# Decode trunk step on one core: key pages of heads 4-7 by plain loads, the other gathers in pairs with time between, GpSimd held to its place

## The chip, the cores and the metric

The kernel is one program on 1 core of one Trainium2 chip. The metric is its time on the device in microseconds (us), from three timed runs; beside them stands one execution that the hardware profiler recorded. In what follows PE is the matmul engine (TensorE), PEld its weight loads, DVE the vector engine, ACT the scalar engine, POOL GpSimd and SP the engine that issues most of the transfers.

## What is computed

One step of a decoder layer, for a prompt of 512 tokens and for 8 samples of 4 tokens, with shared weights in float32. One projection feeds two groups of 8 heads. Group A is native sparse attention (NSA): compressed blocks, selected blocks and a window. Group B is forgetting attention ("fox"). The samples have 1024 past rows each, held in pages of 128 rows that a page table names.

```python
h = rmsnorm(x, norm_in)
q_n, kv_n, gates, z_n, q_f, k_f, v_f, logf, z_f = project(h, w_in, b_gate, b_forget)
...
past_nsa = cache_nsa_kv[page_table].reshape(B, P, 4, NSA_KV_HEADS, HEAD_DIM)
nsa_all = jnp.concatenate([past_nsa, kv_n[:, :, :4]], axis=1)
kc, c_end = compress(nsa_all[:, :, 0], cmp_pe[0], cmp_w[0])
vc, _ = compress(nsa_all[:, :, 1], cmp_pe[1], cmp_w[1])
...
past_fox = cache_fox_kv[page_table].reshape(B, P, 2, FOX_HEADS, HEAD_DIM)
k_all = jnp.concatenate([past_fox[:, :, 0], k_f], axis=1)
v_all = jnp.concatenate([past_fox[:, :, 1], v_f], axis=1)
o_f = fox_block(q_f, q_pos, d_all[:, P:], k_all, v_all, d_all, jnp.arange(P + T))
...
y = x + einsum(concat(o_n * silu(z_n), o_f * silu(z_f)), w_out)
```

## The kernel before

**Tiles and stages.** The projection runs over 61 column tiles of 128 columns (`run_tiles`). Each takes 96 matmuls into the PSUM tiles `pz`: float32 is made of three products of rounded parts, weights `whi` and `wlo` times input `h_hi` and `h_lo`. A weight quarter arrives as `raw` (256 KB, five buffers), ACT writes `whi` from it and DVE writes `wlo`. After the last tile comes the output projection (`run_outputs`, tile `po`), which takes the 16 mixed heads one after the other.

**Streams.** Everything else is a set of generators (`Streams`) that put their instructions between the projection's matmuls. While the program is built, a model of the five engines (`Clock`) keeps a time for each. `pump`, called after every third matmul, lets each generator go on whose last yield is met: a list of tiles that are ready by the model, a flag, or a function. So the order of every engine is fixed when the program is built, and on the chip the engines meet by semaphores alone. `calm` holds a stream back until the model's DMA queue is short.

**The streams that the change touches.** `fox_sample(hh)` handles heads 0-3 (hh = 0), then heads 4-7 (hh = 1). Its `pager` fills pages `fpg` (128 partitions, 4 x 512 elements, two buffers): first 16 key pages, then 16 value pages. A key page is four gathers, each an indirect DMA of 128 rows of 512 elements that POOL issues with indices from `fi`; the gather puts row i + 32a of sample b in partition 32b + i and quarter a. DVE transposes the page into `ft`, and PE makes scores in `accv`. A value page is four plain loads by `load_page`, whose page number comes from a register; samples with an even number go over SP's queue, those with an odd one over POOL's. `compress` makes the compressed keys and values of the samples' pages: `load_rows(u)` gathers 16 sets of rows `crow` (four gathers each, two buffers), set u + 2 as soon as set u has been transposed into `ct`. `nsa()` runs `compress`, `nsa_prompt` and `nsa_sample` in this order; `nsa_sample` loads its pages `spg` in the same way as value pages.

**POOL's queue.** After the index arithmetic POOL issues nothing but gathers and its half of the plain loads. A gather waits on the chip only for its buffer (read by DVE) and, at the start, for one weight quarter (the copy into `gone`). Nothing else ties it to the place that the model gave it.

Of the kernel before, what the change touches and what calls it, by code (L numbers as in the profile page):

```python
# [23 lines left out]
TOK = 544  # L24
FPG = 2
CALM = 4.0
HALF_D = 1024
T_WIN = 28
SETS = 5
# [202 lines left out]
class Streams:  # L232
# [3 lines left out]
    def __init__(self, clock):  # L236
        self.clock = clock
        self.items = []
        self.flags = set()
        self.left = {"tr": 2, "nat": 2}  # L240

    def add(self, gen, front=False, filler=False):
        s = dict(gen=gen, flags=(), at=0.0, test=None, filler=filler)
# [51 lines left out]

    def calm(self, us):
        return lambda: self.clock.queued() <= us

    def after(self, us):
        until = self.clock.t["pe"] + us  # L300
# [28 lines left out]
def dram(ap, offset, dims):  # L329
    return bass.AP(tensor=ap.tensor, offset=ap.offset + offset, ap=dims)  # L330
# [3 lines left out]
def trunk_step(ctx, tc, x_prompt, x_sample, cache_nsa_kv, cache_fox_kv, cache_fox_logf, state_nsa_win,  # L334
# [16 lines left out]
    def gate(side):  # L351
        return lambda: clock.t["pe"] >= clock.gate.get(side, 0.0)
# [98 lines left out]
    nc.vector.memset(ones, 1.0)  # L451
    bias32 = cst.tile([P, 32], F32, name="bias32")
    w_0 = {}


    h_hi = keep.tile([P, KT, TOK], F32R, name="h_hi")
    h_lo = keep.tile([P, KT, TOK], F32R, name="h_lo")
# [468 lines left out]
    def gather(t, tab, idx):  # L926
        nc.gpsimd.indirect_dma_start(out=t, out_offset=None, in_=tab,
                                     in_offset=bass.IndirectOffsetOnAxis(ap=idx, axis=0))
# [191 lines left out]
    def fox_sample(hh):  # L1120
# [7 lines left out]
        def pager():  # L1128
            while at[0] < len(seq):
                yield lambda: at[0] < at[1] + FPG  # L1130
                yield S.calm(CALM)
                kv, bq, kb = seq[at[0]]
                pages[at[0]] = pg = fx.tile([P, 4, 512], F32, name="fpg", bufs=FPG)
                for b in range(4):
                    if kv:
                        load_page(pg[:, b], cache_fox_kv, (bq * 4 + b) * 8 + kb,
                                  lambda c: c[0, :, 1, hs, :].rearrange("p h d -> p (h d)"))
                    else:
                        gather(pg[:, b], dram(cache_fox_kv, 0, [[512, n_pool * 512], [1, 512]]),
                               IX["f"][hh][:, bq * 8 + kb, b:b + 1])  # L1140
                at[0] += 1

        if hh == 0:
            yield ("idx", "x15")
            first = raws[3 + W_RAW]
            yield [first]
            nc.gpsimd.tensor_copy(IX["gone"], first[:, 3, P - 1:])
        S.add(pager())
        qb = fx.tile([P, 4, 4, 64], F32, name="fqb")
        nc.vector.memset(qb, 0.0)  # L1150
# [148 lines left out]
    def compress(pl):  # L1299
# [5 lines left out]
        S.put_nat()  # L1305
        gs, cw = {}, {}

        def load_rows(u):
            if u < 16:
                cg, bh = divmod(u, 2)  # L1310
                gs[u] = pl.tile([P, 4, 512], F32, name="crow", bufs=2)
                for b in range(4):
                    gather(gs[u][:, b], nsa_tab, IX["c"][:, bh * 4 + b, cg:cg + 1])

        def load_w(s):
            if s < 32:
                cg, kv, dp = s // 4, s // 2 % 2, s % 2
                cw[s] = t = pl.tile([P, 2, P], F32, name="cw", bufs=3)
                for d in range(2):
                    load(t[:, d], dram(cmp_w, (kv * 32 + cg * 4) * P * P + (dp * 2 + d) * 32 * P, [[P * P, 4], [P, 32], [1, P]]))  # L1320
        load_rows(0)
        load_w(0)
        load_w(1)
        more = []
        for kv in range(2):
# [13 lines left out]
                                  peT[:, :, kv * 8:kv * 8 + 8].rearrange("p d g -> p g d"))  # L1339
            nc.vector.transpose(m[:, :, :32], cz.rearrange("p g d -> p (g d)"))  # L1340
            yield
        load_rows(1)
        WIDE = 256 + MORE
        pss = [s_tile([P, WIDE]) for _ in range(2)]
        psb = psum.tile([P, 2, 256], F32, name="psb", tag="acc", bufs=1)
# [8 lines left out]
        for step in steps + [None]:  # L1354
            if step:
                cg, bh, kv, dp = step
                u, s = cg * 2 + bh, cg * 4 + kv * 2 + dp
                if bh == 0:
                    load_w(s + 2)
                    yield [cw[s]]  # L1360
                    ws[kv, dp] = pair(pl, [P, 2, P], "cwx", 4)
                    yield from split((*ws[kv, dp], cw.pop(s)))
                n = 256 if bh else WIDE
                X = [x[:, :, :n] for x in pair(pl, [P, 2, WIDE], "cx", 3)]
                yield [gs[u]]
                t = pl.tile([P, 2, WIDE], F32, name="ct", bufs=2)[:, :, :n]
                if bh == 0:
                    cp(t[:, :, 256:], more[kv][:, cg * 4 + dp * 2:cg * 4 + dp * 2 + 2, :])
                nc.vector.transpose(t[:, :, :256].rearrange("p c (a i) -> p a c i", i=32),
                                    gs[u].rearrange("p b (k v d) -> p b k v d", k=2, v=2)[:, :, kv, :, dp * 64:dp * 64 + 64])  # L1370
                yield
                if kv and dp:
                    gs.pop(u)
                    load_rows(u + 2)
                yield from split((*X, t))
                now = step, ws[kv, dp], X
            if prev:
                at, w, x = prev
                for c in range(2):
                    yield [x[1], w[1]]  # L1380
                    products(*at, c, w, x)
            prev = now
# [679 lines left out]
    def index_tiles():  # L2062
# [52 lines left out]
        nc.gpsimd.tensor_scalar(cb_, cb_, 2.0, None, op0=OP.mult)  # L2115
        nc.gpsimd.tensor_tensor(at, steps[:, None, :].to_broadcast([P, 8, 8]), cb_[:, :, None].to_broadcast([P, 8, 8]), op=OP.add)
        nc.gpsimd.tensor_copy(IX["c"], at)
        IX["gone"] = fsk.tile([P, 1], F32, name="gone")
        p2 = IX["p2"] = fsk.tile([64, 2], I32, name="pid2")
        for x in range(2):  # L2120
            nc.gpsimd.tensor_scalar(p2[:, x:x + 1], pid, 2.0, float(x), op0=OP.mult, op1=OP.add)
# [16 lines left out]
    if True:  # L2138
        fsk = pool("fsk")
        fxk = ctx.enter_context(tile_pool("fxk", **side))  # L2140
        fxs = ExitStack()
        fx = fxs.enter_context(tile_pool("fx", **side))
        qs_f = fxk.tile([P, 8, 32], F32, name="qs_f")
        ks_f = fxk.tile([P, 8, 32], F32, name="ks_f")
        ptrow = fsk.tile([1, 64], I32, name="ptrow")

        def nsa():
            yield ("idx", "started", "places")
            with tile_pool("phc") as pl:
                yield from compress(pl)  # L2150
            yield gate("left")
            with tile_pool("phn") as pl:
                yield from nsa_prompt(pl)
            yield gate("left")
            with tile_pool("phs") as pl:
                yield from nsa_sample(pl)
            yield gate("left")
            pl = ctx.enter_context(tile_pool("mxp"))
            MX.update(mx=by_rows(pl.tile([P, 16, TOK], F32, name="mx")), pl=pl, kept=set(), free=4)
            flags.add("mx")  # L2160

        def fox():
            pn = []
            for hh in range(2):
                pn.append((yield from fox_sample(hh)))
            fxs.close()
            yield gate("right")
            with tile_pool("phf", **side) as pl:
                for hh in range(2):
                    S.add(new_values(pl, hh, pn[hh]))  # L2170
                yield from fox_prompt(pl)
                yield ("foxs0", "foxs1")
            flags.add("fox")

        S.add(index_tiles(), front=True)
        S.add(start(), front=True)
        S.add(places())
        S.add(fox_sample_setup())
        S.add(fox())
        S.add(nsa())  # L2180
        for hd in range(16):
            S.add(mix(hd))
            S.add(turn_in(hd))
        S.add(last_stage())
        run_tiles(0, n_in)
        flags.add("in_done")
        S.need("mx")
# [28 lines left out]
```

## Time and profile before

| | us |
|---|---|
| median of 3 runs | 1327.93 (1327.69 to 1328.9) |
| profiled execution | 1329.99 |
| its span, first to last instruction | 1328.3 |
| PE busy in the span | 1272.8 |
| mean granted clock of PE | 0.979 |

PE's two clock states in this trace are full (1.0) and half; the profile's rows give the mean over a stretch. "Busy" of PE counts pipelined matmuls, so a busy PE is not always one at its peak. An idle stretch is put down to the engine or transfer that ended it; "issue" means that the profile shows nothing it waited for.

### The profile page before, as it was taken

How to read it: one execution, taken by the hardware profiler on the slowest of the kernel's cores; microseconds unless marked ns; L12 is line 12 of the kernel's file. 1: busy time of each engine (PE TensorE's matmuls, PEld its weight loads, DVE VectorE, ACT ScalarE, POOL GpSimd, SP SyncE). 2: the span in 40 equal slices, each digit the busy share in tenths (PEclk: the TensorE clock that was granted, in tenths of full speed). 3: DMA queues.
4: the chain of work that ended last, by engine and by line, in shares of the span. 5: the costliest groups of instructions: out<-in, count | busy, mean ns of one | idle time of the engine just before them, and what ended most of it. 6: DMA issues, size and time to landing. Idle time of an engine off the chain costs nothing.

```text
span 1328.3 us, 27189 instructions
## 1 busy us (share of the span) xinstructions
PE 1272.8 (96%) x10097; PEld 1144.2 (86%) x10097; DVE 785.4 (59%) x1979; ACT 540.6 (41%) x1164; POOL 286.1 (22%) x377
## 2 busy tenths in 40 slices
PE   8899988888999999999999999999999999999997
PEld 6899968878988988888998889979899899777786
DVE  6545746666764457767565554876586437345255
ACT  5323312322343224545355553557567524333221
POOL 6400354455241134444001111011200100000000
PEclk9999988899999989999999999999999999999999
DMA  8655767678687888776946878796977785434423
GB/s 212 208 120 138 210 198 217 204 218 235 206 272 230 276 249 253 237 238 209 267 102 192 229 232 188 187 221 194 286 206 183 219 295 170 129 108 132 138 74 135
DMA packets 308053, 266.30 MB, mean 200 GB/s; under 512 B 87174, under 2 KB 255062, under 8 KB 307248
## 3 DMA queue, kind: packets, MB, share of 16 engines
q1 hardware_dynamic: 283968, 188.60, 50.4%
q0 software_dynamic: 23904, 75.84, 18.0%
q8 instruction: 79, 1.29, 0.4%
q14 instruction: 54, 0.44, 0.1%
q10 hardware_dynamic: 48, 0.13, 0.0%
HBM read 236.04 MB, written 36.77 MB: 205 GB/s over the span
## 4 chain that ended last, share of the span: by engine, by line
PE 86%; DVE 3%; issue 3%; DMA 3%; ACT 2%; another core or an unknown queue 2%; SPq 1%; DVEq 0%; ACTq 0%
PE pz L195 51%; PE po L195 15%; PE s L195 5%; PE tr L195 5%; PE accv L195 4%; PE acc L195 3%; PE psb L195 2%; PE accf L195 1%; SPq L195 1%; DVE ft L195 1%; DMA spg<-in_state_nsa_win 1%; DMA raw<-in_w_in 1%; DMA xt<-in_x_prompt 1%; ACT np L195 1%
## 5 line engine op out<-in xcount | busy, mean ns | idle before, releaser
L195 PE MATMUL pz<-h_hi,whi 128*128 128x272 f32 x1920 | 569.0, 296 | 16.6 <-ACT zt L195 9.8
L195 PE MATMUL pz<-h_hi,wlo 128*128 128x272 f32 x1920 | 559.3, 291 | 5.9 <-issue 5.9
L195 PE MATMUL pz<-h_lo,whi 128*128 128x272 f32 x1920 | 559.0, 291 | 5.4 <-issue 5.1
L195 PEld LDWEIGHTS pz<-h_hi,whi 128*128 128x128 f32 x1920 | 367.1, 191 | 31.3 <-issue 18.8
L195 PEld LDWEIGHTS pz<-h_lo,whi 128*128 128x128 f32 x1920 | 367.2, 191 | 9.1 <-issue 8.4
L195 PEld LDWEIGHTS pz<-h_hi,wlo 128*128 128x128 f32 x1920 | 366.9, 191 | 8.1 <-issue 8.0
L195 DVE TENSOR_TENSOR wlo<-raw,whi 128x512 fp32r<-128x512 f32 x275 | 186.3, 679 | 144.1 <-ACT whi L195 137.5
L195 ACT ACTIVATE whi<-raw 128x512 fp32r<-128x512 f32 x275 | 170.8, 625 | 246.3 <-PE pz L195 132.4
L195 POOL DMA_INDIRECT fpg<-in_cache_fox_kv,fi x128 | 131.1, 1024 | 163.8 <-DVE ft L195 97.5
L195 DVE TENSOR_TENSOR zt<-pz,rsb 128x272 f32<-128x272 f32 x86 | 37.9, 440 | 151.6 <-PE pz L195 139.3
L195 POOL DMA_INDIRECT crow<-in_cache_nsa_kv,ci x64 | 66.4, 1038 | 141.2 <-DVE qs_f L195 72.7
L195 PE MATMUL po<-whi,h_hi 128*128 128x512 f32 (+1 forms) x256 | 95.5, 373 | 0.0
L195 PE MATMUL po<-whi,h_lo 128*128 128x512 f32 (+1 forms) x256 | 93.5, 365 | 0.0
L195 PE MATMUL po<-wlo,h_hi 128*128 128x512 f32 (+1 forms) x256 | 93.4, 365 | 0.0
L195 DVE STREAM_TRANSPOSE ft<-fpg 128x1024 f32<-128x1024 f32 x64 | 78.9, 1235 | 9.9 <-remote 5.0
L195 POOL DMA_DIRECT2D spg<-in_cache_nsa_kv x64 | 34.9, 546 | 228.4 <-DVE skt L195 99.3
L195 POOL DMA_DIRECT2D fpg<-in_cache_fox_kv x64 | 34.7, 542 | 223.7 <-PE accv L195 172.0
L195 ACT ACTIVATE cxh<-ct 128x580 fp32r<-128x580 f32 (+1 forms) x64 | 42.1, 658 | 90.1 <-DVE ct L195 53.3
L195 PEld LDWEIGHTS po<-whi,h_hi 128*128 128x128 f32 x256 | 48.1, 188 | 19.7 <-ACT whi L195 7.5
L195 PEld LDWEIGHTS po<-whi,h_lo 128*128 128x128 f32 x256 | 48.2, 188 | 8.5
L195 PEld LDWEIGHTS po<-wlo,h_hi 128*128 128x128 f32 x256 | 48.2, 188 | 7.7
L195 DVE TENSOR_TENSOR cxl<-ct,cxh 128x580 fp32r<-128x580 f32 (+1 forms) x64 | 46.0, 719 | 12.4 <-ACT cxh L195 8.1
(411 smaller groups left out, 1874.3 us busy)
## 6 DMA issues: line engine op xcount, KB each, us to landing
raw<-in_w_in SPq DMA_DIRECT2D x240, 256.0 KB
fpg<-in_cache_fox_kv SPq DMA_DIRECT2D x64, 256.0 KB
fpg<-in_cache_fox_kv POOLq DMA_DIRECT2D x64, 256.0 KB
raw<-in_w_out SPq DMA_DIRECT2D x40, 256.0 KB
spg<-in_cache_nsa_kv POOLq DMA_DIRECT2D x64, 128.0 KB
spg<-in_cache_nsa_kv SPq DMA_DIRECT2D x64, 128.0 KB
out<-in_state_nsa_win SPq DMA_DIRECT2D x32, 254.0 KB
scr_z<-zt SPq DMA_DIRECT2D x28, 272.0 KB
```

The source lines that it names most:

```text
L195: return fn(*a, **k)
```

## The change

Key pages of heads 4-7 come by `load_page`: four loads of 32 partitions x 4 x 512 elements, which put the same rows in the same places. `calm` now holds back only the pages of heads 4-7. The gathers that remain (key pages of heads 0-3 and the rows of `compress`) come in pairs. Ahead of each pair stands `S.spaced`: it lets the pair in when the model's PE time is at least 2.8 us after the pair before, rows of `compress` ahead of key pages, and then calls `mark(j)`, which lets ACT write one column of `tick` and POOL copy it into `gone`. So POOL waits for ACT before each pair. `load_rows` becomes a stream of its own, `rows_in`. `nsa_sample` now also waits for the flag "sampled", set when both halves of the fox sample are done.

```diff
+SPACE = 2.8
...
+    def spaced(self, first=False):
+        self.ahead += first
+        yield lambda: self.clock.t["pe"] >= self.spaced_at and (first or not self.ahead)
+        self.ahead -= first
+        self.spaced_at = self.clock.t["pe"] + SPACE
+        j = self.gathers % 8
+        self.gathers += 1
+        self.mark(j)
...
+    tick = cst.tile([P, 8], F32, name="tick")
+    gone = cst.tile([P, 8], F32, name="gone")
+    clock.parts[tick.tensor.name] = clock.parts[gone.tensor.name] = (8, 1)
+
+    def mark(j):
+        cp(tick[:, j:j + 1], ident[:, j:j + 1])
+        nc.gpsimd.tensor_copy(gone[:, j:j + 1], tick[:, j:j + 1])
+    S.mark = mark
...
         def pager():
             while at[0] < len(seq):
                 yield lambda: at[0] < at[1] + FPG
-                yield S.calm(CALM)
+                if hh:
+                    yield S.calm(CALM)
...
+                    elif hh:
+                        load_page(pg[b * 32:b * 32 + 32], cache_fox_kv, (bq * 4 + b) * 8 + kb,
+                                  lambda c: c[0, :, 0, hs, :].rearrange("(a i) h d -> i a (h d)", i=32))
                     else:
+                        if b % 2 == 0:
+                            yield from S.spaced()
                         gather(pg[:, b], dram(cache_fox_kv, 0, [[512, n_pool * 512], [1, 512]]),
                                IX["f"][hh][:, bq * 8 + kb, b:b + 1])
...
-        def load_rows(u):
-            if u < 16:
+        done = [0]
+
+        def rows_in():
+            for u in range(16):
+                yield lambda: u < done[0] + 2
                 cg, bh = divmod(u, 2)
-                gs[u] = pl.tile([P, 4, 512], F32, name="crow", bufs=2)
+                rows = pl.tile([P, 4, 512], F32, name="crow", bufs=2)
                 for b in range(4):
-                    gather(gs[u][:, b], nsa_tab, IX["c"][:, bh * 4 + b, cg:cg + 1])
+                    if b % 2 == 0:
+                        yield from S.spaced(True)
+                    gather(rows[:, b], nsa_tab, IX["c"][:, bh * 4 + b, cg:cg + 1])
+                gs[u] = rows
...
+                yield lambda: u in gs
                 yield [gs[u]]
...
                     gs.pop(u)
-                    load_rows(u + 2)
+                    done[0] += 1
...
+            yield "sampled"
...
+            flags.add("sampled")
```

How this moves instructions is shown at three places. The first is POOL's queue in the first part of the program, where the pages of heads 0-3 and the rows of `compress` are gathered. Before (`fpg` key pages, `crow` rows of `compress`, `fi_248` and `ci` their indices):

```order
L195 COPY gone<-raw 128x1
L195 DMA fpg<-in_cache_fox_kv,fi_248 128x512 x8
L195 DMA crow<-in_cache_nsa_kv,ci 128x512 x16
L195 DMA fpg<-in_cache_fox_kv,fi_248 128x512 x8
L195 DMA crow<-in_cache_nsa_kv,ci 128x512 x4
```

And now, from the first gathers after the 16 of `crow` on (`tick` is written by ACT):

```order
L196 COPY gone<-tick 128x1
L196 DMA fpg<-in_cache_fox_kv,fi_250 128x512 x2
L196 COPY gone<-tick 128x1
L196 DMA fpg<-in_cache_fox_kv,fi_250 128x512 x2
L196 COPY gone<-tick 128x1
L196 DMA crow<-in_cache_nsa_kv,ci 128x512 x2
```

Eight and four gathers in a row have become twos, with a copy that waits for ACT before each.

The second place is ACT's queue in the same part of the program, now (`cxh` and `cwxh` are the rounded parts of `compress`, `ct` its transposed rows, `zt` a finished projection tile):

```order
L196 ACTIVATE tick<-ident 128x1
L196 ACTIVATE zt<-pz 128x272
L196 ACTIVATE cxh<-ct 128x580
L196 ACTIVATE tick<-ident 128x1
L196 ACTIVATE whi<-raw 128x512
L196 ACTIVATE cwxh<-cw 128x256
```

The ticks stand between the splits of weights and rows, so each is reached only when ACT has done the ones before it; before, the same operations stood there without them.

The third place is SP's queue where the sample's scores of heads 4-7 begin (`fss` is loaded for their softmax, `nat` holds stored rows). Before:

```order
L195 DMA fss<-scr_f 128x1x1024
L195 DMA scr_z<-zt 128x544
L195 DMA raw<-in_w_in 128x4x128 x2
L195 DMA out<-nat 4x32x32
L195 DMA out<-nat 32x16x32
```

And now:

```order
L196 DMA fss<-scr_f 128x1x1024
L196 ISA
L196 DMA fpg<-in_cache_fox_kv 32x4x512
L196 ISA
L196 DMA fpg<-in_cache_fox_kv 32x4x512
L196 DMA raw<-in_w_in 128x4x128
L196 DMA out<-in_state_nsa_win 16x4064
```

Two loads of each key page of heads 4-7 now stand in SP's queue ahead of weights (ISA sets up the register with the page's number); the other two stand in POOL's, where there were 64 gathers in a row.

More of the change, by code (lines that the diff above doesn't have):

```diff
@@ L240, in __init__ @@
         self.left = {"tr": 2, "nat": 2}
+        self.gathers, self.spaced_at, self.ahead = 0, 0.0, 0
     def add(self, gen, front=False, filler=False):
@@ L1146, in fox_sample @@
             yield [first]
-            nc.gpsimd.tensor_copy(IX["gone"], first[:, 3, P - 1:])
+            nc.gpsimd.tensor_copy(gone[:, :1], first[:, 3, P - 1:])
         S.add(pager())
@@ L1320, in load_w @@
                     load(t[:, d], dram(cmp_w, (kv * 32 + cg * 4) * P * P + (dp * 2 + d) * 32 * P, [[P * P, 4], [P, 32], [1, P]]))
-        load_rows(0)
+        S.add(rows_in())
         load_w(0)
@@ L1341, in compress @@
             yield
-        load_rows(1)
         WIDE = 256 + MORE
@@ L2117, in index_tiles @@
         nc.gpsimd.tensor_copy(IX["c"], at)
-        IX["gone"] = fsk.tile([P, 1], F32, name="gone")
         p2 = IX["p2"] = fsk.tile([64, 2], I32, name="pid2")
```

## Prediction, made before the change was run

> **What bounds the kernel now.** I read the page's head and chain first, to see which engine sets the end.
>
> ```profile
> PE 1272.8 (96%) x10097; PEld 1144.2 (86%) x10097; DVE 785.4 (59%) x1979; ACT 540.6 (41%) x1164; POOL 286.1 (22%) x377
> PEclk9999988899999989999999999999999999999999
> PE 86%; DVE 3%; issue 3%; DMA 3%; ACT 2%; another core or an unknown queue 2%; SPq 1%; DVEq 0%; ACTq 0%
> ```
>
> PE is the bound: 1272.8 us busy of a span of 1328.3, so 55.5 us idle, and some slices in which its granted clock is below full. Only these two, idle time and lost clock, can be won. The waits of PE name what ended the idle time; the longest row (us in total, times, longest):
>
> ```profile
> PE pz L195 <- issue: 17.4, 27, 1.2
> ```
>
> It is "issue": PE waited for no semaphore that the profile shows, 27 times before matmuls of the projection (tile pz). No engine and no transfer holds it there, so the next view is the order of time around such a place, first PE, then POOL (GpSimd).
>
> ```profile
> 165.41 0.38 PE L195 MATMUL accv<-ft,fqb 128*32 128x256 f32 x1 [0.30 <-issue]
> 166.15 0.39 PE L195 MATMUL accv<-ft,fqb 128*32 128x256 f32 x1 [0.36 <-issue]
> 167.56 0.38 PE L195 MATMUL accv<-ft,fqb 128*32 128x256 f32 x1 [1.02 <-issue]
> 169.00 0.38 PE L195 MATMUL accv<-ft,fqb 128*32 128x256 f32 x1 [1.06 <-issue]
> ```
>
> ```profile
> 158.65 0.94 POOL L195 DMA_INDIRECT fpg<-in_cache_fox_kv,fi  x1 [12.32 <-DVE ft L195]
> ...
> 173.15 0.95 POOL L195 DMA_INDIRECT crow<-in_cache_nsa_kv,ci  x1 [0.30 <-issue]
> 181.92 0.94 POOL L195 DMA_INDIRECT fpg<-in_cache_fox_kv,fi  x1 [7.82 <-DVE ft L195]
> ```
>
> PE crawls, one matmul in 0.7 to 1.4 us, while POOL issues twelve gathers in a row, 158.65 to 174.1, each 0.94 to 1.35 us with 0.30 us between. The same pairing stands at every long run. The rows below are windows: length, then busy time and count of PE, PEld, DVE, ACT and POOL, granted clock, DMA. The first seven go from the start of a run to where PE is back at full clock; the eighth is the projection alone; the ninth holds three runs of four, the tenth one more run of eight (and a copy).
>
> ```profile
> 49.30:67.00 17.70, 12.31 (x81) 12.09 (x79) 9.34 (x31) 4.76 (x10) 7.96 (x8) 0.81 0.71 203
> 158.60:180.00 21.40, 15.62 (x94) 11.57 (x94) 11.56 (x20) 4.70 (x10) 12.10 (x12) 0.76 0.75 226
> 191.10:207.00 15.90, 12.74 (x95) 11.20 (x94) 8.45 (x15) 5.07 (x13) 8.07 (x8) 0.79 0.71 210
> 219.00:241.10 22.10, 16.48 (x126) 14.54 (x125) 12.67 (x21) 5.38 (x11) 13.43 (x13) 0.85 0.66 201
> 280.40:296.00 15.60, 12.02 (x78) 11.23 (x77) 7.57 (x12) 3.48 (x8) 7.74 (x8) 0.89 0.76 235
> 319.10:337.00 17.90, 14.30 (x101) 12.26 (x94) 7.52 (x13) 3.88 (x9) 8.12 (x8) 0.81 0.68 185
> 473.60:490.30 16.70, 13.84 (x93) 12.44 (x86) 9.53 (x34) 4.38 (x10) 7.98 (x8) 0.80 0.88 264
> 80.00:120.00 40.00, 40.00 (x321) 40.00 (x321) 15.88 (x32) 8.69 (x15) 0.00 (x0) 1.00 0.55 136
> 296.00:318.00 22.00, 22.00 (x192) 20.92 (x192) 16.52 (x26) 8.21 (x17) 12.30 (x12) 1.00 0.78 227
> 30.00:44.00 14.00, 14.00 (x114) 13.92 (x114) 9.46 (x22) 8.87 (x12) 10.63 (x9) 1.00 0.79 237
> ```
>
> All seven hold 8 to 12 gathers without a pause, have an idle PE and a clock of 0.76 to 0.89. The ninth has 12 gathers too, but in three runs of four, and PE is busy for all of its 22 us at full clock. The tenth has a run of eight and no loss; its nine operations took 10.63 us, 1.18 each against 1.00 (7.96 / 8) in the first, so it was slower. So the length of a dense run hurts, not the number of gathers. POOL's order of time in that ninth window shows what pause was enough.
>
> ```profile
> 300.61 0.94 POOL L195 DMA_INDIRECT fpg<-in_cache_fox_kv,fi  x1 [0.30 <-issue]
> 302.92 0.94 POOL L195 DMA_INDIRECT crow<-in_cache_nsa_kv,ci  x1 [1.36 <-DVE ct L195]
> ...
> 307.06 0.95 POOL L195 DMA_INDIRECT crow<-in_cache_nsa_kv,ci  x1 [0.30 <-issue]
> 310.51 1.13 POOL L195 DMA_INDIRECT fpg<-in_cache_fox_kv,fi  x1 [2.50 <-DVE ft L195]
> ```
>
> Pauses of 1.36 and 2.50 us between runs of four were enough; the 0.30 us inside a run is not.
>
> **The change, part by part.** *The long runs.* The seven windows last 17.7 + 21.4 + 15.9 + 22.1 + 15.6 + 17.9 + 16.7 = 127.3 us and hold 81 + 94 + 95 + 126 + 78 + 101 + 93 = 668 matmuls. At the rate of the eighth row, 321 in 40 us or 8.03 per us, they need 83.2 us: 44.1 us are lost. At that of the ninth, 192 in 22 us or 8.73 per us, they need 76.5 us: 50.8 lost. Both ends are close; I take the middle, 47.4. Six of the seven runs become pairs, each behind a small ACT operation that writes tick and a POOL copy that waits for it, 2.8 us of PE work apart at the least. The seventh, at 473.6, holds gathers of heads 4-7, which are gone. A pair lasts about 2.2 us (two of 0.95 and 0.30 between); with 2.8 from pair to pair 0.6 us are left, less than the 1.36 that was enough after four, but after half as many gathers. Runs as short as two do not occur in this trace; the bounds are a full cure (the ninth row) and half a cure, and I take the full one, as the row of four is nearest.
>
> *Short runs of the second key phase.* From 490.3 to 640 heads 4-7 are gathered in runs of four, and PE idles 149.7 - 145.4 = 4.3 us there.
>
> ```profile
> 490.30:640.00 149.70, 145.40 (x1250) 132.24 (x1248) 109.28 (x298) 68.78 (x180) 58.34 (x60) 1.00 0.76 235
> 380.00:480.00 100.00, 100.00 (x804) 88.70 (x803) 48.27 (x115) 31.49 (x64) 23.77 (x35) 1.00 0.83 263
> 840.00:900.00 60.00, 56.87 (x518) 52.37 (x518) 44.25 (x129) 36.32 (x78) 4.41 (x8) 0.97 0.82 199
> ```
>
> The gathers go, and the same bytes come by 64 plain loads, half issued by SP and half by POOL. Where value pages come by plain loads now (380 to 480) PE idles nothing. I take half of the 4.3, that is 2.1; the bounds are 0 and 4.3.
>
> *Plain loads on SP.* Of the 64 new loads 32 stand in SP's queue, each to 32 partitions, and behind a load that waits for its page buffer stand the weights (raw).
>
> ```profile
> SPq L195 <- PE accv L195: 28.3, 11, 6.5
> L195 SPq DMA_DIRECT2D fpg<-in_cache_fox_kv x64: 332/353/1241, 338.5 to 789.3; - x64
> ```
>
> For value pages SP already waits so, up to 6.5 us at a time, and the second row of the fence before shows PE undisturbed: five raw buffers cover it. 32 x 0.353 = 11.3 us of issue on SP over 150 us is hidden by the same cover. The other nearest row is 840 to 900, where SP issues the NSA pages to 32 partitions each: there PE idles 3.1 us in 60. Bounds: 0, and 3.1 x 150 / 60 = 7.8. I take 3.1 as a cost, nearer to the value pages. POOL issues 32 loads where it had 64 gathers, so it has less to do, not more.
>
> *Ticks and copies.* 64 pairs need 64 of each. The nearest ACT row is 245 ns and POOL's copies lie between these two:
>
> ```profile
> L195 ACT ACTIVATE ct<-more 128x68 f32<-128x68 f32 x32 | 7.8, 245 | 0.0
> L195 POOL COPY gone<-raw 128x1 f32<-128x1 f32 x1 | 1.7, 1687 | 7.8 <-DMA raw<-in_w_in 7.8
> L195 POOL TENSOR_SCALAR pid<-pid 64x1 int32<-64x1 int32 x2 | 0.3, 182 | 0.0
> ```
>
> ACT: 64 x 0.245 = 15.7 us, on an engine that is 59% idle; the cover is its waiting for PE (below), and with that gone each tick would delay a split of weights by 0.245. POOL: 64 x 0.182 = 11.6 us, or 64 x 1.687 = 108. I take the small one, since the large one had just come out of a wait for a transfer. Behind a waiting copy stand only the next gathers; who waits for those are the transposes on DVE (ft, ct). Cost on the path: 0, with the other end under the third rival.
>
> *What moves.* Counted in rows of PE's order, the NSA prompt and sample stages come about one projection tile (96 matmuls of pz) later, so less lone projection is left ahead of the output stage. The chain of waits has that stretch in one row (start, us, count):
>
> ```profile
> 1075.70 43.24 PE pz L195 x345
> ```
>
> It hides the mixing of heads, whose loads start there. By the new order some 204 of the 345 are left, 43.24 x 204 / 345 = 25.6 us; the outputs take the 16 heads one by one, so I cost it at nothing. With that cover gone altogether the first output would be late by what the mixing of one head takes, a few us.
>
> Sum against the profiled execution, 1329.99 us: 47.4 + 2.1 - 3.1 = 46.4 won, 1283.6. The median of the runs is 2.06 below that execution, so **1281.5**. The forecast's own range: 50.8 + 4.3 - 0 gives 1273 and 44.1 + 0 - 7.8 gives 1292.
>
> **Rivals.**
>
> ```profile
> L195 POOL DMA_INDIRECT fpg<-in_cache_fox_kv,fi x128 | 131.1, 1024 | 163.8 <-DVE ft L195 97.5
> L195 POOL DMA_INDIRECT crow<-in_cache_nsa_kv,ci x64 | 66.4, 1038 | 141.2 <-DVE qs_f L195 72.7
> q8 instruction: 79, 1.29, 0.4%
> ACT whi L195 <- PE pz L195: 132.4, 61, 11.0
> ```
>
> *Loss by gather, not by run.* If each of the 128 + 64 = 192 gathers in these two groups costs the same 47.4 / 192 = 0.25 us, only the 64 of heads 4-7 help: 15.8 won, 2.1 and 3.1 as above, so 1313. For it speaks that PE's gaps have no named releaser; against it the ninth window, 12 gathers and no loss. The third row above shows that instructions themselves come by DMA, 1.29 MB in 79 packets, 16 KB each. [...]
>
> *Pairs too dense.* Two gathers in 2.8 us are 1.4 us for one, against 1.25 in a run. If 0.6 us of pause restores only half, half of the six runs' loss stays: the seventh lost 16.7 - 93 / 8.03 = 5.1, so (47.4 - 5.1) / 2 = 21 more, 1303.
>
> *Slower: POOL behind its plan.* If a copy costs 1.687 us, a pair takes 2.5 + 1.7 = 4.2 us on POOL where the plan has 2.8, and every tick also waits for the copy eight pairs before, which frees its column. From eight pairs behind, POOL stops ACT, ACT the weight splits, and PE stops. The price: 52 pairs after the first 24 gathers, 1.4 us each, 73 us: 1354. It decides as soon as a copy takes over 0.3 us and the pairs stand dense. Against it: ACT waits 2.2 us for PE on average (132.4 / 61), so the plan has slack at both ends, and POOL is 22% busy.
>
> *The change does nothing.* If the runs only coincide with the crawl, or ticks come so early that POOL still runs through, the time stays at 1324 to 1330.
>
> **How the numbers follow.** Forecast 0.62, loss by gather 0.10, pairs too dense 0.16, slower 0.07, nothing 0.05. The range, 1272 to 1313, holds the forecast and the dense pairs and ends at the loss by gather. 0.2% is about what a measurement of this kernel can tell from no change. Faster 0.88, same 0.05, slower 0.07.
>
> **What the profile will show.** If right: no "issue" row over 5 us among PE's waits, PE busy for about 98% (of its 55.5 us idle the seven windows hold 30.0), PEclk at 9 from slice 2 to slice 38, gathers on POOL in twos with a copy before each. Dense pairs: PE's clock under 1.00 between 120 and 340. POOL behind: ACT waiting for POOL's copies, copies over 1 us. Loss by gather: idle PE spread evenly over 130 to 400. SP's loads too dear: PE waiting for whi or wlo between 470 and 620. The forecast is wrong if PE's idle time stays over 35 us.

## The result, and the profile after

Timed side by side on one chip, the changed kernel took 1299.34 us as the median of four runs (1297.77 to 1300.72), the kernel before 1328.13 (1327.69 to 1328.9): a ratio of 0.9773 (95% interval 0.9750 to 0.9797), 28.8 us won. The likeliest case said 1281.5, so a gain of the named kind came, at six tenths of its size. The rival "pairs too dense" stands nearest, with 1303.

The page of the changed kernel, its busy times, PE's clock by slices and the chain of the end:

```profile
PE 1259.2 (97%) x10097; PEld 1136.4 (88%) x10097; DVE 784.2 (61%) x1979; ACT 552.3 (43%) x1240; POOL 263.2 (20%) x409
PEclk9999999999999999999999999999999999999999
PE 81%; DMA 10%; DVE 3%; ACT 2%; issue 2%; SPq 1%; another core or an unknown queue 0%; DVEq 0%; ACTq 0%
```

Of a span of 1296.1 us PE is idle for 36.9; before it was 55.5. The clock row has no slice under 9 any more, but a tenth is coarse. PE's waits (us in total, times, longest) show that the kind of loss is still there, only smaller:

```profile
PE psb L196 <- issue: 4.9, 4, 1.7
...
PE accv L196 <- issue: 2.7, 4, 1.0
...
PE pz L196 <- issue: 1.3, 2, 0.9
```

Where is it left? The order of time on POOL, and then on PE, at one such place:

```profile
174.95 0.18 POOL L196 COPY gone<-tick 128x1 f32<-128x1 f32 x1 [0.91 <-ACT tick L196]
175.67 0.97 POOL L196 DMA_INDIRECT fpg<-in_cache_fox_kv,fi  x1 [0.53 <-issue]
...
178.13 0.20 POOL L196 COPY gone<-tick 128x1 f32<-128x1 f32 x1
...
180.71 0.19 POOL L196 COPY gone<-tick 128x1 f32<-128x1 f32 x1
...
183.29 0.20 POOL L196 COPY gone<-tick 128x1 f32<-128x1 f32 x1
...
184.93 0.95 POOL L196 DMA_INDIRECT crow<-in_cache_nsa_kv,ci  x1 [0.30 <-issue]
```

```profile
183.27 0.29 PE L196 MATMUL pz<-h_lo,whi 128*128 128x272 f32 x1
184.02 0.37 PE L196 MATMUL pz<-h_hi,wlo 128*128 128x272 f32 x1 [0.46 <-issue]
186.12 0.28 PE L196 MATMUL psb<-cxh,cwxh 128*128 128x256 f32 x1 [1.73 <-issue]
187.53 0.28 PE L196 MATMUL psb<-cxl,cwxh 128*128 128x256 f32 x1 [1.13 <-issue]
```

The copies stand between the pairs, as meant, but only the first waited for its tick. The others follow 2.6 us apart, which is what two gathers and a copy take POOL. Four pairs make a run of 8 gathers without a pause, and 8 us after its start PE crawls as before, with its clock at 0.90 in this stretch (window: length, then busy time and count of PE, PEld, DVE, ACT, POOL, granted clock, DMA):

```profile
175.00:192.00 17.00, 13.68 (x94) 13.21 (x93) 11.46 (x19) 6.24 (x18) 10.79 (x15) 0.90 0.79 234
```

That is the sign that the prediction named for dense pairs; over the whole of 120 to 340, where it looked for it, the clock is 0.98. For the whole trace, the answer on the copies (count, duration in ns, what they waited for in us and times):

```profile
L196 POOL COPY gone<-tick x64: 182/204/2182, 30.3 to 368.8; 128x1 f32<-128x1 f32 x64
...
  ACT tick L196: 140.8, 21
```

21 of 64 copies waited for a tick. For the other 43 the tick was there already, and POOL went straight on.

### The profile page after: what moved, and what is told of

It is laid out like the page before. It is cut to its first block, busy times and chain, and to the rows that moved or that the text cites. A ratio compares the mean times of both kernels' runs of the same rounds, so it can differ in the third digit from the quotient of the medians.

```text
span 1296.1 us, 27480 instructions
## 1 busy us (share of the span) xinstructions
PE 1259.2 (97%) x10097; PEld 1136.4 (88%) x10097; DVE 784.2 (61%) x1979; ACT 552.3 (43%) x1240; POOL 263.2 (20%) x409
## 3 DMA queue, kind: packets, MB, share of 16 engines
q8 instruction: 79, 1.29, 0.4%
## 4 chain that ended last, share of the span: by engine, by line
PE 81%; DMA 10%; DVE 3%; ACT 2%; issue 2%; SPq 1%; another core or an unknown queue 0%; DVEq 0%; ACTq 0%
PE pz L196 47%; PE po L196 15%; PE s L196 4%; PE accv L196 4%; PE tr L196 4%; DMA fpg<-in_cache_fox_kv 4%; PE acc L196 3%; DMA raw<-in_w_in 2%; PE psb L196 2%; DMA nz<-scr_z 2%; SPq L196 1%; PE accf L196 1%; DMA scr_o<-fot 1%; DMA xt<-in_x_prompt 1%; DVE ft L196 1%
## 5 line engine op out<-in xcount | busy, mean ns | idle before, releaser
L196 POOL DMA_DIRECT2D fpg<-in_cache_fox_kv x96 | 52.7, 549 | 334.5 <-PE accv L196 163.9
L196 DVE TENSOR_TENSOR zt<-pz,rsb 128x272 f32<-128x272 f32 x76 | 33.4, 439 | 128.8 <-PE pz L196 122.7
L196 POOL DMA_INDIRECT fpg<-in_cache_fox_kv,fi x64 | 68.4, 1069 | 17.0 <-issue 14.2
L196 ACT ACTIVATE zt<-pz 128x272 f32<-128x272 f32 x45 | 17.9, 397 | 98.2 <-PE pz L196 95.1
```

The lines of the kernel that those rows point to most:

```text
L196: return fn(*a, **k)
```

## Experiments

Six sets of runs were made, each on one chip with the kernel before beside it. They fall into two kinds, those in which the kernel before takes about 1266 us and those in which it takes 1327 to 1336, and without this no later number can be read. "The crawl" is the loss of PE's time beside runs of gathers, as the prediction describes it:

| set | chip's number | kernel before, median us | kernels in it |
|---|---|---|---|
| A | not recorded | 1328.13 | the change (the result above) |
| B | 11 | 1336.17 | pairs 4.0 us apart, pairs 5.6 us apart, no tick |
| C | 3 | 1266.45 | a run of gathers, a run of plain loads, all keys plain, fours at 7.0 us |
| D | 7 | 1266.55 | the kernel before, the change |
| E | 5 | 1266.52 | two runs in the projection, plain loads only |
| F | 3 | 1327.53 | fours at 7.0 us with two runs in the projection |

**Is the crawl a matter of the kernel alone? (set D)** Both kernels unchanged.

> The kernel before, unchanged, for its profile. It took 1336 us as the median on one chip and 1266 on another. Theory (PE's crawl beside long runs of gathers is a matter of the chip as well as of the kernel): where it takes about 1266, its profile shows the same seven runs of 8 to 12 gathers with 0.30 us between on POOL, but PE idle under 4 us in them at full clock; where it takes 1326 to 1340, the crawl at all seven. Rival (on the faster chip the gathers themselves come apart, are shorter or wait for landings, so there are no dense runs): other runs on POOL than in the first profile, under 8 in a row.

> The changed kernel, unchanged. Theory: where the kernel before takes about 1266 there is no crawl to cure, and the ratio is 0.997 to 1.004; where it takes 1326 to 1340 the ratio is 0.975 to 0.980 as measured first. Rival (the change gains by the plain loads or by the moved stages, on any chip): a ratio under 0.99 on both.

Before: 1268.67 us. The change: 1274.80 against 1266.55, a ratio of 1.0059 (1.0041 to 1.0078), a little above the 1.004 that theory allowed. Where the kernel before takes 1266 us, the change is 0.6% slower. The profile of the kernel before in this set, first and last gather of a run on POOL, and the window of that stretch:

```profile
151.29 0.94 POOL L195 DMA_INDIRECT fpg<-in_cache_fox_kv,fi  x1 [11.69 <-DVE ft L195]
...
188.26 0.95 POOL L195 DMA_INDIRECT fpg<-in_cache_fox_kv,fi  x1 [0.30 <-issue]
```

```profile
151.00:190.00 39.00, 39.00 (x343) 36.87 (x343) 32.02 (x52) 14.97 (x32) 29.70 (x28) 1.00 0.92 278
```

28 gathers in a row, more than anywhere in the first trace, and PE is busy for all 39 us at full clock. So a long run of gathers is not enough: something that differs from set to set must come to it. The same window of four executions, in the order set A before, set A after, set D before, set D after:

```profile
49.00:490.00 441.00, 408.49 (x3191) 377.45 (x3190) 256.29 (x511) 131.85 (x274) 148.46 (x160) 0.95 0.72 214
```

```profile
49.00:490.00 441.00, 426.16 (x3445) 398.78 (x3445) 273.14 (x569) 149.45 (x369) 165.29 (x218) 0.98 0.77 225
```

```profile
49.00:490.00 441.00, 439.48 (x3677) 412.73 (x3677) 301.60 (x644) 160.57 (x350) 171.67 (x184) 1.00 0.82 245
```

```profile
49.00:490.00 441.00, 438.77 (x3658) 412.79 (x3657) 289.64 (x615) 162.27 (x400) 168.13 (x224) 1.00 0.83 239
```

At D's rate, 3677 / 441 = 8.34 matmuls per us, set A's kernel before is short by 486 matmuls or 58 us; the change by 213 of 3658, 26 us.

**Do gathers alone do it? (sets C, E, F)** Extra transfers into a small tile that nobody reads, in the lone projection, where POOL otherwise stands still. Set C has 16 gathers in one kernel, 16 plain loads in another; E has both in one; F has both in the kernel of fours (below).

```diff
+            for t, n in ((90.0, 16), (122.0, 24)):
+                yield lambda: clock.t["pe"] >= t
+                yield from S.spaced(True)
+                for i in range(n):
+                    if n == 16:
+                        gather(dump[:, i % 6], dram(cache_fox_kv, 0, [[4, n_pool * 512], [1, 4]]),
+                               IX["f"][0][:, i // 4, i % 4:i % 4 + 1])
+                    else:
+                        nc.gpsimd.dma_start(dump[:, i % 6], dram(cache_fox_kv, i * P * 2048, [[2048, P], [1, 4]]))
```

> The changed kernel with 16 extra gathers in a row (128 rows of 16 bytes each, into a tile that nobody reads), behind a tick, in the stretch from 71 to 95 us, where POOL stands still and PE does nothing but the projection at full clock without a gap. Theory (a dense run of GpSimd gathers by itself makes PE crawl, and the bytes are not the reason: 16 such gathers carry 33 KB where 16 of the kernel's carry 4 MB): after 5 to 8 us of the run PE crawls until about 2 us after its end, 4 to 10 us idle, one or more stretches of half clock of 3.41 us, the run takes 16 x 1.25 = 20 us or less. Rival (the data of the gathers, 2 KB for each row, or what stands beside them in the sampled stage starves PE): no gap over 0.3 us and full clock.

> As the run before, but with 16 plain loads of the same shape (128 rows of 16 bytes) issued by POOL in a row at the same place. Theory (what hurts is the gather on GpSimd, not that POOL issues transfers): PE loses under 1 us there at full clock. Rival (any long run of transfers from POOL does it, through descriptors or small packets): the same crawl as with gathers, 4 us or more.

> The changed kernel with two extra runs of transfers on POOL, each behind a tick, in the lone projection between 70 and 120 us: 16 gathers of 128 rows of 16 bytes in a row (about 78 to 98), then 24 plain loads of the same shape in a row (about 102 to 116). On the chip on which the kernel before took 1266 neither made a gap. Theory (on a chip on which the kernel before takes 1326 to 1340, a run of gathers alone is enough): 4 to 10 us of PE idle and half clock in the first stretch, under 1 us in the second. Rival 1 (the 2 KB rows, or the other work of that stage, are needed too): no gap in either. Rival 2 (any run of transfers on POOL): both. On a chip on which the kernel before takes about 1266: no gap in either, and the question stays open.

> The changed kernel with four gathers for each tick at 7.0 us (as in the run of fours) and the two extra runs of transfers in the lone projection (16 gathers of 128 rows of 16 bytes at about 78 to 98, 24 plain loads at about 108 to 123). On a chip on which the kernel before takes 1326 to 1340: theory (runs of four with a pause behind are too short to starve PE, a run of 16 is enough by itself) 3 us idle or less between 130 and 340, 4 to 10 us idle and half clock between 78 and 100, none between 105 and 125, ratio 0.962 to 0.975. Rival 1 (the 2 KB rows or the work beside them are needed): no gap between 78 and 100. Rival 2 (fours hurt): over 8 us idle between 130 and 340. On a chip where it takes about 1266: no gap in any of these, ratio 1.000 to 1.008, and both stay open.

C and E are sets without the crawl, and no gap came beside the extra runs: 1269.81 us (gathers) and 1272.71 (plain loads) in C, 1274.86 with both in E. Set F has the crawl. Windows of F: ahead of the gathers, around them, around the plain loads; then the window around the gathers in set E:

```profile
66.00:78.00 12.00, 12.00 (x99) 11.75 (x99) 6.45 (x23) 2.37 (x4) 0.00 (x0) 0.99 0.40 106
78.00:102.00 24.00, 15.48 (x112) 14.97 (x112) 7.14 (x13) 2.63 (x6) 15.92 (x17) 0.83 0.35 74
122.00:138.00 16.00, 16.00 (x130) 16.00 (x129) 10.26 (x21) 6.79 (x18) 13.02 (x25) 1.00 0.44 107
```

```profile
78.00:102.00 24.00, 24.00 (x194) 24.00 (x193) 7.59 (x15) 5.07 (x8) 16.66 (x17) 1.00 0.65 148
```

In F the 16 gathers cost 8.5 us of idle PE and a clock of 0.83, 82 matmuls less than in E; the 24 plain loads cost nothing. The shortest stretches of half clock in the kernel before of set A last 3.41 us; one stands at 0.50 from 292.21 to 295.62, with 1.00 on both sides. The gathers carried 16 x 128 x 16 bytes, 33 KB. So in this trace, one execution, a run of gathers on POOL is enough to cause the loss, without the data, the pages or the other stages. What POOL, PE, ACT, DVE and SP do meanwhile, in the same stretch of F:

```profile
81.95 0.98 POOL L196 DMA_INDIRECT dump<-in_cache_fox_kv,fi  x1 [0.16 <-issue]
...
100.89 0.94 POOL L196 DMA_INDIRECT dump<-in_cache_fox_kv,fi  x1 [0.30 <-issue]
```

```profile
87.71 0.28 PE L196 MATMUL pz<-h_hi,wlo 128*128 128x272 f32 x1
...
89.21 0.29 PE L196 MATMUL pz<-h_hi,wlo 128*128 128x272 f32 x1
92.51 0.37 PE L196 MATMUL pz<-h_hi,whi 128*128 128x272 f32 x1 [3.01 <-DVE zt L196]
...
94.25 0.43 PE L196 MATMUL pz<-h_hi,wlo 128*128 128x272 f32 x1
100.18 0.59 PE L196 MATMUL pz<-h_hi,whi 128*128 128x272 f32 x1 [5.50 <-issue]
```

```profile
97.58 0.63 ACT L196 ACTIVATE whi<-raw 128x512 fp32r<-128x512 f32 x1 [9.32 <-remote]
```

```profile
91.92 0.44 DVE L196 TENSOR_TENSOR zt<-pz,rsb 128x272 f32<-128x272 f32 x1 [7.17 <-remote]
99.68 0.44 DVE L196 TENSOR_TENSOR zt<-pz,rsb 128x272 f32<-128x272 f32 x1 [7.32 <-remote]
100.04 0.68 DVE L196 TENSOR_TENSOR wlo<-raw,whi 128x512 fp32r<-128x512 f32 x1
```

```profile
82.27 18.84 SPq L196 DMA_DIRECT2D raw<-in_w_in  x4
```

```profile
100.75 0.37 SPq L196 DMA_DIRECT2D raw<-in_w_in  x1
```

PE stops 7.5 us into the run (89.21 + 0.29 - 81.95), and POOL's own gathers keep their 0.94 us. But PE's two stops are waits for DVE. `pz` has two buffers, one for each half of a column tile, so PE can write a half of the next tile only when DVE's `zt` has read the old one. The first stop is put down to that by name. The second ends 0.06 us after the second `zt` (99.68 + 0.44), though the profile names nothing there; between the two PE runs 12 matmuls, one half's share, without a gap.

DVE was late. PE had finished the two halves at 88.00 and 89.50 (the ends of the matmuls at 87.71 and 89.21), and DVE began to read them 3.9 and 10.2 us later, after standing for 7.2 and 7.3 us ("remote": no releaser in the trace). In set E, beside the same gathers, such a read begins 0.04 us after PE is done (98.35 after 98.31). ACT stands for 9.3 us in the same way, where in this stretch of E it never waits more than 2.4. SP does not stop by itself either: the last of its four weight loads goes out at 100.75, right behind the `wlo` (100.04 + 0.68) with which DVE frees a `raw` buffer. So DVE and ACT stand still without a reason that the trace shows, and PE and SP wait for DVE.

**Is 2.8 us too dense? (set B)** One line each: `SPACE = 4.0`, `SPACE = 5.6`.

> The changed kernel with 4.0 us from pair to pair instead of 2.8. In the changed kernel POOL's pairs still follow each other every 2.6 to 2.9 us (copy included) in eleven groups of 6 to 10 gathers, and PE keeps 14.3 us idle between 49 and 340. Theory (2.8 is no pause, POOL itself needs that long for a pair): with about 1.2 us of real pause PE's idle time between 49 and 400 falls under 5 us and the time to 1279-1289. Rival 1 (each gather costs its part whatever the pause): 1297-1302. Rival 2 (the gathers are cured, but the NSA stages come later and the end pays it): idle gone before 400, yet 1292-1305, with new waits of PE after 900.

> The changed kernel with 5.6 us from pair to pair. Theory: the stall is gone as at 4.0 or more so, under 3 us idle between 49 and 500, 1277-1289 if the later stages have room. Rival 1 (cost by gather): 1297-1302. Rival 2 (the gathers now take 64 x 5.6 = 358 us, later stages are late): slower than the kernel with 4.0, 1290-1315.

Pairs at 4.0: 1295.65 us, ratio 0.9696 (0.9673 to 0.9720). At 5.6: 1321.39, ratio 0.9878 (0.9856 to 0.9900). First 4.0, then 5.6, the stretch of the gathers and that of the later stages:

```profile
49.00:490.00 441.00, 436.64 (x3593) 412.95 (x3592) 285.70 (x616) 170.75 (x421) 163.54 (x212) 1.00 0.77 222
...
640.00:1120.00 480.00, 463.35 (x3844) 416.26 (x3843) 278.64 (x802) 250.49 (x517) 52.27 (x96) 0.98 0.78 209
```

```profile
49.00:490.00 441.00, 438.63 (x3609) 426.07 (x3610) 291.29 (x625) 174.43 (x427) 150.13 (x185) 1.00 0.71 200
...
640.00:1120.00 480.00, 438.68 (x3765) 388.75 (x3764) 272.57 (x761) 229.36 (x482) 63.34 (x116) 0.95 0.83 214
```

And the later stages in set A, before and after:

```profile
640.00:1120.00 480.00, 476.26 (x4117) 440.62 (x4114) 292.21 (x890) 255.88 (x558) 49.96 (x92) 1.00 0.77 212
```

```profile
640.00:1120.00 480.00, 472.49 (x3971) 429.82 (x3971) 292.91 (x884) 261.20 (x567) 50.26 (x92) 0.99 0.75 204
```

Both halves came out. In the gather stretch PE's idle time falls from 14.8 us (441 - 426.16) to 4.4 and 2.4, at full clock, so the loss there hangs on the pause, and "loss by gather" falls. In the later stages it grows from 7.5 us to 16.7 and 41.3: the gathers now hold back the NSA stages, which meet the end of the projection with less left to hide them. Of the 5888 matmuls of `pz`, 1701 are still to come at the first load of a page `spg` in the change, 1567 at 4.0 and 1027 at 5.6. In us, the time at 4.0 missed theory's 1279 to 1289 and lies in rival 2's range, and at 5.6 it lies above every range. But B's kernel before is 8 us slower than A's. Scaled by the ratios to A's 1328.1, 4.0 gives 1287.8, which is theory's, and 5.6 gives 1311.9, which is rival 2's. So the time alone does not decide, and the windows do: they show theory's cure and rival 2's price side by side. By the ratios 4.0 is faster than 2.8 and 5.6 slower; the change itself was not timed in set B.

**Is the hold needed? (set B)** Without `self.mark(j)`: the plan spaces the pairs, nothing ties POOL to it.

> The changed kernel without the tick on ACT and the copy on POOL: the gathers keep their place in the plan, in pairs 2.8 us apart, but nothing holds POOL to it. Theory (POOL runs ahead whenever its waits allow, so the plan alone makes no pause): runs of 8 to 12 gathers with 0.30 us between come back, PE idle between 49 and 340 back over 22 us, 1308-1322. Rival (order in the plan is what counts, hold is not needed): 1296-1302.

1327.20 us, ratio 0.9937 (0.9907 to 0.9967): theory's case, a little above its range in us, in a set whose kernel before is 8 us slower than A's. PE in the gather stretch is nearly where it was before the change:

```profile
49.00:490.00 441.00, 410.05 (x3226) 377.03 (x3224) 254.61 (x508) 132.79 (x275) 140.28 (x156) 0.95 0.73 211
```

The hold is worth the step from 0.9937 to 0.9773, as far as ratios of sets B and A may be compared. The 0.6% that stay without it are put down to the plain loads; they were not run alone in a set with the crawl.

**Runs of four (sets C, F).** One tick for four gathers, 7.0 us apart.

```diff
-SPACE = 2.8
+SPACE = 7.0
...
-                    if b % 2 == 0:
+                    if b == 0:
                         yield from S.spaced(True)
```

> The changed kernel with four gathers for each tick and 7.0 us from tick to tick: a mean rate of 3.5 us for two gathers, between 2.8 and 4.0, in runs of four with a pause of some 2 us. Theory (a run must last some 5 to 7 us before PE starves, the pause behind it is what counts): 49 to 340 nearly cured (idle under 5 us), ratio 0.966 to 0.973. Rival (runs of four hurt by themselves): idle over 10 us there, ratio above 0.977.

The same with 8.0 us from tick to tick, meant to stand beside pairs at 4.0, has no time: the program so built deadlocks. Set C, without the crawl, could not answer for 7.0: 1268.27 us, ratio 1.0017 (1.0004 to 1.0030), nearest to the kernel before of all changed ones there. In set F, with the extra runs, it took 1306.14 us, ratio 0.9843 (0.9809 to 0.9877). That misses theory's 0.962 to 0.975, also without the 8.5 us of the extra gathers. Two windows differ:

```profile
140.00:208.00 68.00, 67.47 (x572) 64.80 (x571) 53.39 (x99) 24.66 (x60) 35.70 (x40) 1.00 0.78 228
210.00:292.00 82.00, 74.66 (x592) 66.88 (x590) 52.57 (x83) 26.10 (x63) 43.30 (x50) 0.98 0.76 223
```

In the first POOL issues eight runs of four, and PE idles 0.5 us; in the second, five runs of eight, since POOL was late and found the next tick there, and PE idles 7.3. That is rival 2's number with theory's cause: over the whole stretch fours did hurt, but where two of them had grown together. Counted from POOL's and PE's rows of the six traces with the crawl, from 45 us on (a run ends at a pause of 1 us; PE's idle time from its start to the next run's, whatever ended it):

| gathers in the run | 2 | 4 | 6 | 8 | 10 | 12 | 16 |
|---|---|---|---|---|---|---|---|
| runs | 59 | 81 | 11 | 26 | 2 | 4 | 1 |
| mean idle PE, us | 0.04 | 0.12 | 0.66 | 2.08 | 4.25 | 5.56 | 8.52 |

The means grow with the run, but length is not all: the eights alone go from 0 to 6.2 us, and the eight at 30 us in the kernel before, ahead of this count, cost nothing.

**What do the plain loads cost? (set E)** The kernel before with `load_page` for the key pages of heads 4-7 alone.

> The kernel before with only the plain loads for the key pages of heads 4-7, no pairs and no ticks. By the steps of the prediction: 5.1 us of the seventh run and 2.1 us of the short runs won, 3.1 us paid on SP's queue, 4 us won or a ratio of 0.997, on a chip where the kernel before takes 1326 to 1340. Rival (the plain loads are the part that gains, by the whole second key phase: 490 to 640 lost 24 us against about 14 where there is no crawl): 10 us or more won, 0.992 or less. On a chip where it takes about 1266: nothing to win there, the cost of the loads alone, a ratio of 1.000 to 1.006.

1270.31 us, ratio 1.0026 (1.0012 to 1.0040): the case without a crawl, 3.8 us of cost by the medians.

**All key pages plain (set C).** Heads 0-3 too, with `calm`, and the rest of the gathers at 4.0 us.

> The changed kernel with the key pages of heads 0-3 by plain loads as well (with the same look at the load of the queues as for heads 4-7), so that only the 64 gathers of crow are left, in pairs 4.0 us apart. Theory (half the gathers gone, the others with real pauses, and the NSA stages not held back as in the kernel with 4.0 and all gathers, since 32 pairs x 4.0 = 128 us instead of 256): PE idle between 49 and 400 under 5 us and no later stages late, 1268-1284 against 1328 of before, a ratio of 0.955 to 0.967. Rival (plain loads in 32 partitions cost PE or the weights' queue more than they save): ratio 0.970 or more, with waits of PE for whi, wlo, ft or fpg between 30 and 300.

1316.71 us, ratio 1.0387 (1.0358 to 1.0415): the rival. This is no crawl: set C has none, and there is no "issue" among PE's waits and no "remote" among DVE's. SP's queue and POOL's loads, then DVE and PE, at the longest:

```profile
291.91 2.94 SPq L196 DMA_DIRECT2D fpg<-in_cache_fox_kv  x2
...
295.40 13.35 SPq L196 DMA_DIRECT2D out<-nat  x10
```

```profile
295.15 1.19 POOL L196 DMA_DIRECT2D fpg<-in_cache_fox_kv  x2
```

```profile
306.41 1.25 DVE L196 STREAM_TRANSPOSE ft<-fpg 128x1024 f32<-128x1024 f32 x1 [9.38 <-DMA fpg<-in_cache_fox_kv]
```

```profile
308.29 0.58 PE L196 MATMUL psb<-cxl,cwxh 128*128 128x256 f32 x1 [6.47 <-DVE cxl L196]
```

DVE waits 9.4 us for a page, and behind DVE's page stands what PE needs next. The last loads of `fpg` ahead of that wait were issued by 296.34 (295.15 + 1.19), so the page landed late, 10 us after its issue, and was not issued late. Ten stores of projection tiles stand right behind it in SP's queue and hold that for 13 us; the next page's loads come after them. From 49 to 490 the DMA engines are busy for 0.86 of the time, against 0.82 in D's kernel before. That the page was late for this reason is likely, not shown.

## Why the prediction was right and wrong

**What bounds the kernel, and where it loses: right, for sets with the crawl; how it loses, only in part.** PE is the bound and loses time beside long runs of gathers, and set F shows a run of gathers to be a cause there. What the prediction could not see from one trace is that the loss is absent in half of the sets. What it could have seen is that other engines stop as well. It said that no engine holds PE at these places, but two more rows of the waits in the kernel before, ACT's and PE's, say otherwise:

```profile
ACT zt L195 <- remote: 14.9, 2, 10.4
...
PE pz L195 <- ACT zt L195: 9.8, 2, 5.4
```

ACT itself stood without a releaser. The two waits of PE for it lie in the first and the fourth of the seven windows, 9.8 of their 30.0 us of idle time, and all of the first window's (17.70 - 12.31).

**The size of the loss: too small.** The seven windows were put at 47.4 us (44.1 to 50.8) and the short runs after 490 at 2.1. Sets A and D differ by 1328.1 - 1266.6 = 61.6 us for the same program, if all of this is the crawl. From 49 to 490 alone PE is short by 58, some 11 more than the seven windows were given.

**The step that failed: "with 2.8 from pair to pair 0.6 us are left", and the full cure taken for it.** The 0.6 came from a pair of 2.2 us, without the copy and without the pause behind the second gather; the rival on POOL behind its plan already counted 2.5. In the trace two gathers and the copy take POOL 2.6 us, which leaves 0.2; and a tick that comes late, or two in a bunch, leaves nothing: 43 of 64 copies did not wait. Of 61.6 us, 1299.3 - 1274.8 = 24.5 remain, so 60% was cured. The rival "pairs too dense" said a half, and its mechanism is the one that came. The prediction saw that 0.6 is less than the 1.36 that was enough, but let the shorter run outweigh it and took the row of four as the nearest; the runs show that without a real pause pairs join to runs of 6 to 10. Pairs at 4.0 us show the step's other half to be right, that a real pause cures.

**Plain loads on SP, 3.1 us: right in size**, 3.8 measured where no crawl hides it. Where the crawl is, the loads seem to gain more than they cost (the 0.6% with no tick), through gathers that are gone.

**Ticks, copies and moved stages at nothing: wrong by a few us.** Set D gives 8.2 us for the whole change, so these cost some 8.2 - 3.8 = 4.4, an estimate across two sets. A copy takes 0.20 us as foreseen. With wider spacing the moved stages become dear: 41 us idle between 640 and 1120 at 5.6. The cover of the later stages, put at nothing here, is the price of every further pause.

**Sum.** 61.6 of crawl, less 24.5 left, less 8.2 paid, is the 28.8 measured, where the prediction had 47.4 + 2.1 - 3.1. The first sum comes out by construction, since its terms are differences of the four medians of sets A and D. Two errors worked against each other: the loss was put some 12 us too small, and the cure taken as full where 24.5 us stayed. That 1299 lies in the range at all is owed to its upper end, which was drawn for the rivals; the forecast's own range ended at 1292.

**The marks.** PE busy for 98%: 97. No "issue" row over 5 us: so, by a hair (4.9). PEclk at 9: so. Gathers in twos with a copy before each: so in the order, but not in time. PE idle over 35 us was to mean that the forecast is wrong: it is 36.9. Loss spread evenly over the gathers: no, it stands beside runs of 6 to 10. POOL behind its plan with ACT waiting for copies over 1 us: no wait of ACT for `gone` in the trace, and one copy of 64 over 1 us. SP's loads making PE wait for `whi` or `wlo`: none among PE's waits.

**The rival that the change is slower** was priced by a mechanism that did not come. The slower case exists nonetheless, by 0.6%, in set D, where there is no crawl to cure.

## What to carry to other kernels

A pause that is planned between transfers must exceed what the issuing engine itself needs for them (here 2.6 us for a pair), and it holds only if that engine has to wait for it; look at how many of the holds were waited for. A gain that cures a stall without a releaser should be timed in several sets of runs, on several chips, with the kernel before beside it: here the same two programs stand at 0.977 and at 1.006. When the engine that bounds the kernel stands idle, look also at what the engines that it waits for were doing: they may be what stopped (in set F DVE and ACT, for up to 7.3 and 9.3 us). Plain loads added where the transfers are already dense can land late, here 10 us after their issue with the DMA engines busy for 0.86 of the time, and then all that stands behind their reader waits (here PE, for 6.5 us).

## What the runs showed of the hardware

The same program took 1266 us in three sets and 1327 to 1336 in three, and chip number 3 stands in a set of each kind, so the number alone does not decide; the records don't say whether it was the same machine. In set F, one of the sets of 1327 to 1336, a run of 16 GpSimd gathers cost PE 8.5 us in 20 for 33 KB of data, from 7.5 us on, while 24 plain loads from the same queue cost nothing (PE was busy for all of the 16 us around them). DVE and ACT stood still, up to 7.3 and 9.3 us, and PE (3.0 and 5.5 us) and SP waited for DVE.

What holds DVE and ACT stayed open, and so did whether PE is ever held by itself: in set F it ran 12 matmuls at once between two waits for DVE, while in the crawl of the first trace it went one by one, a matmul in 0.7 to 1.4 us, with "issue" between. The pages of both kernels in set A show 79 packets of instructions (1.29 MB), with 55.5 us of idle PE in one and 36.9 in the other, so their number does not go with the loss. Nothing was tried that tells a late signal from a late instruction.

No version was found that beats both kernels in both kinds of sets: pairs at 4.0 us were the fastest with the crawl (0.9696), the kernel before without it. Fours at 7.0 us without the extra runs were not timed with the crawl.
